# Weight halves in one tile, and one operand distance for every pass of a width

## The chip, the cores and the metric

The kernel runs on one core of a Trainium2 chip. The time is the device time of one execution in microseconds (us). The kernel before takes 2028.38 us, the median of three runs (2024.63 to 2029.26). The profile is of one execution on the chip. The engines are PE (TensorE, matrix products; PEld is its weight load), DVE (VectorE), ACT (ScalarE), POOL (GpSimd) and SP, which issues the transfers.

## The reference

One layer of a streaming encoder on 2048 tokens of width 1024, all float32: an RMSNorm, one input projection, two groups of heads, an output projection added to the input, a final RMSNorm.

```python
u = rmsnorm(h, norm_g[l])
proj = jnp.einsum('bsd,de->bse', u, w_in[l])
(q, k, v, o_pre, z_m, i_pre, f_pre,
 glu_a, glu_g, z_c) = jnp.split(proj, split_idx, axis=-1)
...
hm = mlstm_chunkwise(q, k, v, i_pre, f_pre)          # 4 heads of 256, matrix memory
hm = jax.nn.sigmoid(o_pre.astype(jnp.float32)) * hm
... # norm per head, times silu(z_m)
c = glu_a * jax.nn.sigmoid(glu_g)
... # causal depthwise convolution of width 31, LayerNorm, silu, times silu(z_c)
mix = jnp.concatenate([hm, c.astype(x.dtype)], axis=-1)
h = h + jnp.einsum('bse,ed->bsd', mix, w_out[l])
```

The input projection has 8 x 1024 + 8 columns, the output projection takes 2048 to 1024. These two are nearly all the work of PE.

## The kernel before

**Products in three passes.** To keep float32 accuracy each operand is split into a high half (rounded to the type fp32r) and a low half (the rest). A product of a weight slab and an activation tile is then three passes on PE: high weight with high activation, high weight with low activation, low weight with high activation (`products`, lines 324 to 353). Every pass is a weight load of a 128x128 stationary operand and a matmul that streams the moving operand past it, both read from SBUF.

**Units.** The tokens are done in two halves of 1024. In each half the projection is a list of units (`seq`), each of 256 columns of weights: `g` (convolution gate), `v`, `o`, `z`, `q`, `k` for four heads and `c`. A unit runs over eight blocks of 128 of the inner dimension. Units `g`, `q`, `k`, `c` (kind "fm", line 336) have the weights stationary and stream 512 tokens: 512 columns a pass. Units `o`, `z`, `v` (kind "tm2", line 343) have the tokens stationary and stream 256 weight columns. The first `v` unit of a half (kind "tm") streams 264 columns. The output projection (kind "tm", line 350) has the mixed tokens stationary and streams 512 weight columns, 8 units of 16 blocks, 12 passes a block.

**Where the operands lie.** An activation tile holds both halves one behind the other; `up` has 8 buffers of 2064 float32 (8256 bytes) a partition (`utiles`, line 271). The weight halves lie in two tiles, `wh` and `wl`, of 528 float32 (2112 bytes), four buffers each (`w_prep_`, line 213). 8256 and 2112 are both 64 more than a multiple of 256, so the place of a tile in a row of 256 bytes goes on by 64 bytes from buffer to buffer. In the built program activation tile j (counted modulo 8) begins at 24960 + 8256 x ((8 - j) mod 8), `wh` of slab i (counted modulo 4) at 91008 + 2112 x ((4 - i) mod 4), `wl` of it 8448 bytes further. Modulo 256 that is 128 - 64j for both halves of an activation tile and 128 - 64i for both halves of a slab. Columns within a tile are offsets of 512 or 1024 bytes in the units of 256 and 512 columns. So what is streamed and what is loaded stand 64 x (j - i) modulo 256 bytes apart where the weights are streamed, 64 x (i - j) where the tokens are, and all four distances (0, 64, 128, 192) take turns.

**Preparing a slab.** SP loads it (`w_load`), ACT writes the high half, POOL subtracts to get the low half, three slabs ahead of PE.

**The other work.** After the unit `k` of a head its eight chunks of 128 tokens (`mlstm`, `chunk`) run beside the later units, in steps s0 to s3: s0 makes the decayed scores `w` on DVE (line 633) from `sk` of PE and splits them, s1 does the products `num` and `kv` on PE (line 601), and the squares `sq` on ACT (line 699), s2 and s3 scale and transpose. The convolution is 31 taps of 128x1024 on DVE (line 787). A scheduler with a timeline simulation sets the order of the instructions on every engine; pools decide what must wait for a buffer to come free. A buffer of `bufs=1` that is shared under one tag makes each user wait for the one before.

Of the kernel before, what the change touches and what calls it, by code (L numbers as in the profile page):

```python
# [14 lines left out]
F32 = mybir.dt.float32  # L15
F32R = mybir.dt.float32r
# [3 lines left out]
P = 128  # L20
# [4 lines left out]
HD = 256  # L25
L = 128
NCH = HT // L
# [12 lines left out]
def hybrid_block_kernel(  # L40
# [14 lines left out]
    PUMP = 0.5  # L55
    WARM = 16

    PAD, ODD = 8, 0

    def pool(name, bufs, **kw):  # L60
        return ctx.enter_context(tc.tile_pool(name=name, bufs=bufs, **kw))
# [129 lines left out]
    wsrc = []  # L191
# [21 lines left out]
    def w_prep_(i):  # L213
        r, n = raws[i // 2]
        odd = wsrc[i // 2][2]
        s = r[:, (i % 2) * n : (i % 2 + 1) * n]
        hi = wp.tile([P, 528], F32R, tag="wh", name=f"wh{i}")
        lo = wp.tile([P, 528], F32R, tag="wl", name=f"wl{i}")
        hi, lo = hi[:, odd : odd + n], lo[:, odd : odd + n]
        nc.scalar.copy(hi, s)  # L220
        nc.gpsimd.tensor_tensor(out=lo, in0=s, in1=hi.bitcast(F32), op=ALU.subtract)  # L221
        wtile[i] = (hi, lo)
# [46 lines left out]
        return ps  # L269

    def utiles(key):
        odd = ODD if key[0][0] == "m" else 0
        both = up.tile([P, 2064], F32R, tag="u", name=f"u_{key[0]}_{key[1]}")
        h_, l_ = both[:, odd : odd + 1024], both[:, odd + 1024 : odd + 2048]
        uh[key], ul[key] = h_, l_
        return h_, l_

# [282 lines left out]
    def mlstm(hf, h):  # L560
# [46 lines left out]
        def chunk(c):  # L607
            tb, cc = c // 4, c % 4
            q, k = q_t[h, tb], k_t[h, tb]
            nm_ = f"{hf}_{h}_{c}"  # L610
            first = hf == 0 and c == 0
            sl = slice(cc * P, (cc + 1) * P)
            last = hf == 1 and c == NCH - 1
            v = [v_t[h, c // 2][:, i, c % 2, :] for i in range(2)]
            sg = oz_t[h, c // 2][:, 0, c % 2, :]
            sz = oz_t[h, c // 2][:, 1, c % 2, :]
            t = {}

            def s0():
                nm, ee = dec[tb]  # L620

                tc.keep_in_program_order(
                    nc.scalar.activation(ee[:, cc], ee[:, cc], AF.Exp, bias=a[:, h, c : c + 1])
                )
                sk = tp.tile([P, 512], F32, tag="tp", name=f"sk_{nm_}")
                for d in range(2):
                    nc.tensor.matmul(sk[:, :P], k[:, d, sl], q[:, d, sl], start=d == 0, stop=d == 1)

                if not last:
                    for d in range(2):  # L630
                        nc.tensor.transpose(sk[:, (d + 1) * P : (d + 2) * P], k[:, d, sl], ident)  # L631
                w = mlp.tile([P, P], F32, tag="w", name=f"w_{nm_}", bufs=1)
                nc.vector.scalar_tensor_tensor(  # L633
                    out=w, in0=sk[:, :P], scalar=rc[:, c : c + 1], in1=ee[:, cc], op0=ALU.mult, op1=ALU.mult
                )
                if not last:
                    kw = mlp.tile([P, 2, HD], F32R, tag="kw", name=f"kw_{nm_}")
                    wac = wa[:, h, c : c + 1]
                    nc.scalar.activation(kw[:, 0], sk[:, P : P + HD], AF.Identity, scale=wac)  # L639
                    nc.vector.scalar_tensor_tensor(  # L640
                        out=kw[:, 1], in0=sk[:, P : P + HD], scalar=wac, in1=kw[:, 0].bitcast(F32),
                        op0=ALU.mult, op1=ALU.subtract,
                    )
                    t["kw"] = kw
                t["w"] = halves(w, [P], "ws", nm_)
                if not first:
                    tc.keep_in_program_order(
                        nc.scalar.activation(nm[:, cc], nm[:, cc], AF.Exp, bias=bc[:, 0, h, c : c + 1])
                    )
                    qs = mlp.tile([P, 2, P], F32, tag="qs", name=f"qs_{nm_}", bufs=1)  # L650
                    nc.vector.tensor_tensor(
                        out=qs, in0=q[:, :, sl], in1=nm[:, cc : cc + 1, :].broadcast_to([P, 2, P]), op=ALU.mult
                    )
                    t["qs"] = halves(qs, [2, P], "qss", nm_)

            def state(d):
                if last:
                    return
                kv = acc.tile([P, 512], F32, tag="acc", name=f"kv_{nm_}_{d}")
                sd = slice(d * P, (d + 1) * P)  # L660
                kw = t["kw"]
                products3(kv[:, :VW], (kw[:, 0, sd], kw[:, 1, sd]), v, True, True)
                if first:
                    nc.vector.tensor_copy(cs[:, d], kv[:, :VW])
                else:
                    nc.vector.scalar_tensor_tensor(  # L666
                        out=cs[:, d], in0=cs[:, d], scalar=so[:, h, c : c + 1],
                        in1=kv[:, :VW], op0=ALU.mult, op1=ALU.add,
                    )
                if c == NCH - 1:  # L670
                    if d == 1:
                        nc.sync.dma_start(csc[h], cs)
                else:
                    state_split(d, nm_)

            def s1():
                num = acc.tile([P, 512], F32, tag="acc", name=f"num_{nm_}")
                products3(num[:, :VW], t["w"], v, True, first)
                if not first:
                    qh, ql = t["qs"]  # L680
                    for d in range(2):
                        products3(num[:, :VW], (qh[:, d], ql[:, d]), chl[d], False, d == 1)
                state(0)

                dn = sp.tile([P, 1], F32, tag="dn", name=f"dn_{nm_}")
                dc = num[:, HD : HD + 1]
                nc.vector.tensor_scalar(
                    out=dn, in0=dc, scalar1=-1.0, scalar2=en[:, h, c : c + 1], op0=ALU.mult, op1=ALU.max
                )
                nc.vector.tensor_tensor(out=dn, in0=dn, in1=dc, op=ALU.max)  # L690
                nc.vector.reciprocal(dn, dn)
                hm = mlp.tile([P, HD + 1], F32, tag="hm", name=f"hm_{nm_}")
                nc.gpsimd.memset(hm[:, HD:], EPS ** 0.5 * HD ** 0.5)
                nc.vector.scalar_tensor_tensor(
                    out=hm[:, :HD], in0=num[:, :HD], scalar=dn, in1=sg, op0=ALU.mult, op1=ALU.mult
                )
                sq = mlp.tile([P, HD + 1], mybir.dt.bfloat16, tag="sq", name=f"sq_{nm_}", bufs=1)
                ss = sp.tile([P, 1], F32, tag="ss", name=f"ss_{nm_}")
                nc.scalar.activation(sq, hm, AF.Square, scale=HD ** -0.5, accum_out=ss)  # L699
                nc.gpsimd.tensor_tensor(out=ss, in0=ss, in1=nhalf[:, 0:1], op=ALU.pow)  # L700
                t["hm"], t["ss"] = hm, ss

            def s2():
                state(1)
                hm = t["hm"][:, :HD]
                nc.vector.scalar_tensor_tensor(
                    out=hm, in0=hm, scalar=t["ss"], in1=sz, op0=ALU.mult, op1=ALU.mult
                )

            def s3():  # L710
                hm = t["hm"]
                mt = tp.tile([P, 512], F32, tag="tp", name=f"mt_{nm_}")
                for d in range(2):
                    nc.tensor.transpose(mt[:, d * P : (d + 1) * P], hm[:, d * P : (d + 1) * P], ident)  # L714
                if cc % 2 == 0:
                    dec["mo"] = k2p.tile([P, 2, 256], F32, tag="k2", name=f"mo_{nm_}")
                mo = dec["mo"]
                for d in range(2):
                    nc.scalar.activation(
                        mo[:, d, (cc % 2) * P : (cc % 2 + 1) * P], mt[:, d * P : (d + 1) * P],  # L720
                        AF.Identity, scale=col(V_MG, 2 * h + d),
                    )
                if cc % 2 == 1:
                    nc.sync.dma_start(
                        mixs[2 * hf + tb][:, 2 * h : 2 * h + 2, (cc - 1) * P : (cc + 1) * P], mo
                    )

            for i, fn in enumerate((s0, s1, s2, s3)):
                slots[SP * c + STG[i]].insert(0, fn)
# [191 lines left out]
    for hf in range(2):  # L921
# [7 lines left out]
        for u in s:  # L929
# [3 lines left out]
                        wsrc.append((wv0[g], 528, 0))  # L933
            else:
                for g in range(2):
                    wsrc.append((wu[WID[u], g], 512, 0 if u[0] in "ozv" else ODD))
    for b in range(4):
        for nn in range(2):
            for g in range(8):
# [16 lines left out]
    u_rstd(0)  # L956

    for hf in range(2):
        gt = gp.tile([P, NCH, 8], F32, tag="g_gt", name=f"gt{hf}", bufs=2)
        key = f"u{hf}"  # L960

        def opnd(kc, key=key):
# [164 lines left out]
```

## Time and profile before

| | |
|---|---|
| median of three runs | 2028.38 us |
| the profiled execution: its time, its span | 2027.2 us, 2025.5 us |
| PE busy, share of the span | 1994.9 us, 98% |
| weight loads (PEld) busy | 1748.2 us, 86% |
| DVE busy | 1430.9 us, 71% |
| ACT, POOL busy | 828.3 us, 801.2 us |
| mean granted clock of PE | 0.994 |

The 1.7 us between time and span lie before the first and after the last instruction. A matmul's own duration overlaps with the next one's (395 ns each for 512 columns, though one starts about every 230 ns), so what a pass costs is read from the distance of starts in the timeline, not from the mean duration.

### The profile page before, as it was taken

How to read it: one execution, taken by the hardware profiler on the slowest of the kernel's cores; microseconds unless marked ns; L12 is line 12 of the kernel's file. 1: busy time of each engine (PE TensorE's matmuls, PEld its weight loads, DVE VectorE, ACT ScalarE, POOL GpSimd, SP SyncE). 2: the span in 40 equal slices, each digit the busy share in tenths (PEclk: the TensorE clock that was granted, in tenths of full speed). 3: DMA queues.
4: the chain of work that ended last, by engine and by line, in shares of the span. 5: the costliest groups of instructions: out<-in, count | busy, mean ns of one | idle time of the engine just before them, and what ended most of it. 6: DMA issues, size and time to landing. Idle time of an engine off the chain costs nothing. (4 is left out here: it accounts for less than half of the span.)

```text
span 2025.5 us, 29786 instructions
## 1 busy us (share of the span) xinstructions
PE 1994.9 (98%) x11562; PEld 1748.2 (86%) x11562; DVE 1430.9 (71%) x1915; ACT 828.3 (41%) x1703; POOL 801.2 (40%) x740
## 2 busy tenths in 40 slices
PE   8999999999999999999999999999999999999998
PEld 7998998899899888888789879988998888788886
DVE  5598887689579755546799998977895658723231
ACT  5133532443343245535445225324423555543332
POOL 4532432343243232534333323423322326556464
PEclk9999999999999999999999999999999999999999
DMA  4211121112122233335311211211221566766452
GB/s 150 70 62 53 58 74 42 63 48 72 44 68 72 75 110 112 114 115 165 101 53 43 70 50 58 74 53 52 68 69 53 161 225 206 265 206 230 150 183 94
DMA packets 85837, 204.11 MB, mean 101 GB/s; under 512 B 7296, under 2 KB 40256, under 8 KB 85696
## 3 DMA queue, kind: packets, MB, share of 16 engines
q1 hardware_dynamic: 85696, 202.21, 30.5%
q8 instruction: 91, 1.49, 0.3%
q14 instruction: 50, 0.41, 0.1%
HBM read 159.15 MB, written 43.03 MB: 100 GB/s over the span
## 5 line engine op out<-in xcount | busy, mean ns | idle before, releaser
L221 POOL TENSOR_TENSOR wl<-wr,wh 128x512 fp32r<-128x512 f32 (+1 forms) x392 | 612.2, 1567 | 857.8 <-ACT wh L220 830.2
L336 PE MATMUL gm<-u_u,wh 128*128 128x512 f32 x2560 | 810.3, 395 | 1.8 <-DVE oz L451 0.9
L787 DVE SCALAR_TENSOR_TENSOR y<-c,vec,y 128x1024 f32<-128x1024 f32 x480 | 708.8, 1477 | 9.5
L336 PEld LDWEIGHTS gm<-u_u,wh 128*128 128x128 f32 x2560 | 477.3, 188 | 105.9 <-DVE oz L451 1.3
L336 PE MATMUL gm<-u_u,wl 128*128 128x512 f32 x1280 | 501.5, 394 | 0.0
L220 ACT CAST wh<-wr 128x512 fp32r<-128x512 f32 (+1 forms) x392 | 241.2, 619 | 598.4 <-PE gm L336 212.1
L343 PE MATMUL gm<-wh,u_u 128*128 128x256 f32 x2816 | 461.0, 282 | 5.5 <-DVE oz L451 3.4
L343 PEld LDWEIGHTS gm<-wh,u_u 128*128 128x128 f32 x2816 | 389.3, 190 | 7.2 <-DVE oz L451 3.6
L350 PE MATMUL gm<-wh,u_m 128*128 128x512 f32 x1024 | 319.7, 396 | 2.2 <-ACT wh L220 2.2
L336 PEld LDWEIGHTS gm<-u_u,wl 128*128 128x128 f32 x1280 | 240.9, 188 | 51.6 <-POOL wl L221 0.2
L343 PE MATMUL gm<-wl,u_u 128*128 128x256 f32 x1408 | 283.9, 282 | 0.0
L350 PEld LDWEIGHTS gm<-wh,u_m 128*128 128x128 f32 x1024 | 192.9, 189 | 46.6 <-ACT wh L220 2.5
L343 PEld LDWEIGHTS gm<-wl,u_u 128*128 128x128 f32 x1408 | 217.8, 190 | 0.1
L350 PE MATMUL gm<-wl,u_m 128*128 128x512 f32 x512 | 199.4, 396 | 0.5 <-POOL wl L221 0.5
L350 PEld LDWEIGHTS gm<-wl,u_m 128*128 128x128 f32 x512 | 96.5, 189 | 23.2 <-POOL wl L221 0.9
L700 POOL TENSOR_TENSOR ss<-ss,nhalf 128x1 f32<-128x1 f32 x64 | 53.5, 836 | 135.5 <-ACT sq L699 128.5
L1019 DVE TENSOR_TENSOR ht<-gm,ht 128x512 f32<-128x512 f32 x32 | 21.4, 688 | 118.5 <-PE gm L350 118.5
L281 DVE TENSOR_TENSOR u_m<-mr,u_m 128x1024 fp32r<-128x1024 f32 x32 | 43.9, 1371 | 76.6 <-ACT u_m L280 76.6
L633 DVE SCALAR_TENSOR_TENSOR w<-sk,rs,ee 128x128 f32<-128x128 f32 x64 | 22.1, 345 | 89.1 <-PE sk L631 84.4
L601 PE MATMUL kv<-v,kw 128*128 128x258 f32 x360 | 73.3, 289 | 0.6 <-DVE cs L666 0.6
L666 DVE SCALAR_TENSOR_TENSOR cs<-cs,g_so,kv 128x258 f32<-128x258 f32 x112 | 53.4, 477 | 24.8 <-PE kv L601 24.7
L639 ACT ACTIVATE kw<-sk,g_wa 128x256 fp32r<-128x256 f32 x60 | 28.3, 472 | 86.6 <-DVE w L633 86.6
(208 smaller groups left out, 2105.5 us busy)
## 6 DMA issues: line engine op xcount, KB each, us to landing
wr<-in_wu SPq DMA_DIRECT2D x123, 512.0 KB, 3.6
wr<-in_wo SPq DMA_DIRECT2D x64, 512.0 KB, 3.6
mr<-mixs SPq DMA_DIRECT2D x32, 512.0 KB, 4.5
ysc<-y SPq DMA_DIRECT2D x16, 512.0 KB, 2.6
mixs<-mo SPq DMA_DIRECT2D x32, 256.0 KB, 2.1
zsc<-zc SPq DMA_DIRECT2D x32, 256.0 KB, 2.1
ly<-ysc SPq DMA_DIRECT2D x16, 512.0 KB, 5.0
lz<-zsc SPq DMA_DIRECT2D x16, 512.0 KB, 5.7
```

The lines of the kernel that those rows point to most:

```text
L220: nc.scalar.copy(hi, s)
L221: nc.gpsimd.tensor_tensor(out=lo, in0=s, in1=hi.bitcast(F32), op=ALU.subtract)
L281: nc.vector.tensor_tensor(out=l_, in0=src, in1=h_.bitcast(F32), op=ALU.subtract)
L336: nc.tensor.matmul(ps[i], wt[:, o + cb * P : o + (cb + 1) * P], at[:, tb * 512 : (tb + 1) * 512], start=st, stop=sp_,)
L343: nc.tensor.matmul(ps[i][:, t2 * 256 : (t2 + 1) * 256], at[:, t * P : (t + 1) * P], wt[:, o : o + ncol], start=st and t2 == 0, stop=sp_, s ...
L350: nc.tensor.matmul(ps[i][:, :ncol], at[:, t * P : (t + 1) * P], wt[:, o : o + ncol], start=st, stop=sp_,)
L601: nc.tensor.matmul(ps, x_, y_, start=start and i == 0, stop=stop and i == 2)
L633: nc.vector.scalar_tensor_tensor(out=w, in0=sk[:, :P], scalar=rc[:, c : c + 1], in1=ee[:, cc], op0=ALU.mult, op1=ALU.mult)
L639: nc.scalar.activation(kw[:, 0], sk[:, P : P + HD], AF.Identity, scale=wac)
L666: nc.vector.scalar_tensor_tensor(out=cs[:, d], in0=cs[:, d], scalar=so[:, h, c : c + 1], in1=kv[:, :VW], op0=ALU.mult, op1=ALU.add,)
L700: nc.gpsimd.tensor_tensor(out=ss, in0=ss, in1=nhalf[:, 0:1], op=ALU.pow)
L787: tc.keep_in_program_order(nc.vector.scalar_tensor_tensor(out=y, in0=c[:, j + i * H2 : j + (i + 1) * H2], scalar=col(V_CW, b * CW + j), in1=y,
```

## The change

Both halves of a slab now lie in one tile `w` of 1152 float32 (4608 bytes, 18 x 256), the low half 2048 bytes behind the high half (2304 in the 264-column unit). The activation tile has 2048 float32 (8192 bytes, 32 x 256). In the built program activation tiles begin at 24960 + 8192n and weight tiles at 90496 + 4608n: all of them at 128 modulo 256. The units that stream 256 weight columns put their weights 48 float32 (192 bytes) into the tile. So in every pass of 512 columns the streamed and the loaded operand stand 0 modulo 512 bytes apart, and in every pass of 256 columns 192 modulo 512 (the streamed one ahead). In the first `v` unit it is 0 or 32 modulo 256.

Besides, `sq` of a chunk takes the one buffer of `w`, and the gate tile `gt` has one buffer in place of two. The scores tile `w` is one float32 longer.

```diff
-    PAD, ODD = 8, 0
+
+    PAD, ODD = 8, 48
...
-        hi = wp.tile([P, 528], F32R, tag="wh", name=f"wh{i}")
-        lo = wp.tile([P, 528], F32R, tag="wl", name=f"wl{i}")
-        hi, lo = hi[:, odd : odd + n], lo[:, odd : odd + n]
+        both = wp.tile([P, 1152], F32R, tag="w", name=f"w{i}")
+        o2 = 576 if n == 528 else odd + 512
+        hi, lo = both[:, odd : odd + n], both[:, o2 : o2 + n]
...
-        odd = ODD if key[0][0] == "m" else 0
-        both = up.tile([P, 2064], F32R, tag="u", name=f"u_{key[0]}_{key[1]}")
-        h_, l_ = both[:, odd : odd + 1024], both[:, odd + 1024 : odd + 2048]
+        both = up.tile([P, 2048], F32R, tag="u", name=f"u_{key[0]}_{key[1]}")
+        h_, l_ = both[:, :1024], both[:, 1024:]
...
-                w = mlp.tile([P, P], F32, tag="w", name=f"w_{nm_}", bufs=1)
+                w = mlp.tile([P, P + 1], F32, tag="w", name=f"w_{nm_}", bufs=1)[:, :P]
...
-                sq = mlp.tile([P, HD + 1], mybir.dt.bfloat16, tag="sq", name=f"sq_{nm_}", bufs=1)
+                sq = mlp.tile([P, HD + 2], mybir.dt.bfloat16, tag="w", name=f"sq_{nm_}", bufs=1)[:, : HD + 1]
...
-                    wsrc.append((wu[WID[u], g], 512, 0 if u[0] in "ozv" else ODD))
+                    wsrc.append((wu[WID[u], g], 512, ODD if u[0] in "ozv" else 0))
...
-        gt = gp.tile([P, NCH, 8], F32, tag="g_gt", name=f"gt{hf}", bufs=2)
+        gt = gp.tile([P, NCH, 8], F32, tag="g_gt", name=f"gt{hf}")
```

Every engine has as many instructions as before; the scheduler sets some of them in another order, most by a few places. One place is the second half, head 0, chunks 5 and 6 (`_1_0_5`, `_1_0_6`), on DVE. Before:

```order
L687 TENSOR_SCALAR dn_1_0_5_10621<-num_1_0_5_10602,g_en1_9379 128x1
L408 SCALAR_TENSOR_TENSOR v_1_1_1_10929<-gm_172_1_10539,rs_1_8272,v_1_1_1_10929 128x256
L633 SCALAR_TENSOR_TENSOR w_1_0_6_10669<-sk_1_0_6_10664,rs_1_8272,ee_1_0_1_10160 128x128
...
L640 SCALAR_TENSOR_TENSOR kw_1_0_6_10671<-sk_1_0_6_10664,g_wa1_9381,kw_1_0_6_10671 128x256
L592 TENSOR_TENSOR wsl_1_0_6_10675<-w_1_0_6_10669,wsh_1_0_6_10674 128x128
...
L694 SCALAR_TENSOR_TENSOR hm_1_0_5_10625<-num_1_0_5_10602,dn_1_0_5_10621,oz_1_0_2_9299 128x256
L787 SCALAR_TENSOR_TENSOR y_1_1_10163<-c_1_1_9007,vec_150,y_1_1_10163 128x1024
L706 SCALAR_TENSOR_TENSOR hm_1_0_5_10625<-hm_1_0_5_10625,ss_1_0_5_10629,oz_1_0_2_9299 128x256
```

Now:

```order
L691 RECIPROCAL dn_1_0_5_10445<-dn_1_0_5_10445 128x1
L787 SCALAR_TENSOR_TENSOR y_1_1_9992<-c_1_1_8856,vec_150,y_1_1_9992 128x1024
L694 SCALAR_TENSOR_TENSOR hm_1_0_5_10449<-num_1_0_5_10426,dn_1_0_5_10445,oz_1_0_2_9144 128x256
L787 SCALAR_TENSOR_TENSOR y_1_1_9992<-c_1_1_8856,vec_150,y_1_1_9992 128x1024
L633 SCALAR_TENSOR_TENSOR w_1_0_6_10492<-sk_1_0_6_10487,rs_1_8137,ee_1_0_1_9989 128x128
L706 SCALAR_TENSOR_TENSOR hm_1_0_5_10449<-hm_1_0_5_10449,ss_1_0_5_10453,oz_1_0_2_9144 128x256
L787 SCALAR_TENSOR_TENSOR y_1_1_9992<-c_1_1_8856,vec_150,y_1_1_9992 128x1024
L640 SCALAR_TENSOR_TENSOR kw_1_0_6_10494<-sk_1_0_6_10487,g_wa1_9225,kw_1_0_6_10494 128x256
L592 TENSOR_TENSOR wsl_1_0_6_10498<-w_1_0_6_10492,wsh_1_0_6_10497 128x128
```

The scores `w` of chunk 6 stood ahead of `hm` of chunk 5, from which `sq` of chunk 5 is made; now they stand behind it.

The second place is POOL, where the low halves of slabs 32 to 34 are made (the brackets name the engines and queues an instruction waits for). Before:

```order
L221 TENSOR_TENSOR wl32_1579<-wr16_1504,wh32_1578 128x512 [waits DMAHW0_49,PE_49,Activation_49]
L221 TENSOR_TENSOR wl33_1609<-wr16_1504,wh33_1608 128x512 [waits PE_49,Activation_49]
L221 TENSOR_TENSOR wl34_1642<-wr17_1576,wh34_1641 128x512 [waits DMAHW1_49,PE_49,Activation_49]
```

Now:

```order
L222 TENSOR_TENSOR w32_1546<-wr16_1474,w32_1546 128x512 [waits DMAHW0_49,Activation_49]
L222 TENSOR_TENSOR w33_1575<-wr16_1474,w33_1575 128x512 [waits Activation_49]
L222 TENSOR_TENSOR w34_1607<-wr17_1544,w34_1607 128x512 [waits DMAHW1_49,Activation_49]
```

POOL no longer waits for PE there: the ACT cast ahead of it takes over the wait, and waits for the last pass that reads the low half of the buffer's former slab, one pass later than the last that reads its high half.

## Rows read from the trace of the kernel before

**Rows 1.** The page: busy time, share of the span and instructions of each engine.

```profile
PE 1994.9 (98%) x11562; PEld 1748.2 (86%) x11562; DVE 1430.9 (71%) x1915; ACT 828.3 (41%) x1703; POOL 801.2 (40%) x740
```

**Rows 2.** Groups of PE by line and shape: busy time, mean ns, idle before.

```profile
L336 PE MATMUL gm<-u_u,wh 128*128 128x512 f32 x2560 | 810.3, 395 | 1.8 <-DVE oz L451 0.9 <-DVE g L759 0.3 <-DVE u_u L293 0.3
L336 PE MATMUL gm<-u_u,wl 128*128 128x512 f32 x1280 | 501.5, 394 | 0.0
L343 PE MATMUL gm<-wh,u_u 128*128 128x256 f32 x2816 | 461.0, 282 | 5.5 <-DVE oz L451 3.4 <-ACT oz L438 1.2 <-DVE v L408 0.8
L350 PE MATMUL gm<-wh,u_m 128*128 128x512 f32 x1024 | 319.7, 396 | 2.2 <-ACT wh L220 2.2
L343 PE MATMUL gm<-wl,u_u 128*128 128x256 f32 x1408 | 283.9, 282 | 0.0
L350 PE MATMUL gm<-wl,u_m 128*128 128x512 f32 x512 | 199.4, 396 | 0.5 <-POOL wl L221 0.5
```

**Rows 3.** Timeline of PE in the output projection: start, length, instruction.

```profile
1862.75 1.76 PE L350 MATMUL gm<-wh,u_m 128*128 128x512 f32 x7
1864.35 0.84 PE L350 MATMUL gm<-wl,u_m 128*128 128x512 f32 x3
1865.03 0.39 PE L350 MATMUL gm<-wh,u_m 128*128 128x512 f32 x1
...
1865.48 0.63 PE L350 MATMUL gm<-wh,u_m 128*128 128x512 f32 x2
...
1868.28 0.63 PE L350 MATMUL gm<-wh,u_m 128*128 128x512 f32 x2
...
1873.86 0.62 PE L350 MATMUL gm<-wh,u_m 128*128 128x512 f32 x2
...
1876.65 0.63 PE L350 MATMUL gm<-wh,u_m 128*128 128x512 f32 x2
...
1879.42 0.63 PE L350 MATMUL gm<-wh,u_m 128*128 128x512 f32 x2
```

**Rows 4.** Timeline of PE in a 256-column unit of the first half.

```profile
468.12 0.62 PE L343 MATMUL gm<-wh,u_u 128*128 128x256 f32 x4
...
470.17 0.63 PE L343 MATMUL gm<-wh,u_u 128*128 128x256 f32 x4
...
472.99 0.63 PE L343 MATMUL gm<-wh,u_u 128*128 128x256 f32 x4
...
475.83 0.63 PE L343 MATMUL gm<-wh,u_u 128*128 128x256 f32 x4
...
478.68 0.63 PE L343 MATMUL gm<-wh,u_u 128*128 128x256 f32 x4
...
481.41 0.64 PE L343 MATMUL gm<-wh,u_u 128*128 128x256 f32 x4
...
484.24 0.64 PE L343 MATMUL gm<-wh,u_u 128*128 128x256 f32 x4
...
487.12 0.63 PE L336 MATMUL gm<-u_u,wh 128*128 128x512 f32 x2
```

**Rows 5.** Window: length; busy us (count) of PE, PEld, DVE, ACT, POOL; clock, DMA.

```profile
1000.00:1250.00 250.00, 240.10 (x1458) 212.69 (x1457) 233.05 (x308) 96.16 (x218) 87.45 (x83) 0.99 0.17 55
```

**Rows 6.** Timeline, two pairs of a w on DVE and the sq before it on ACT.

```profile
1033.02 0.34 DVE L633 SCALAR_TENSOR_TENSOR w<-sk,rs,ee 128x128 f32<-128x128 f32 x1
...
1037.86 0.42 ACT L699 ACTIVATE sq<-hm 128x257 bf16<-128x257 f32 x1 [1.18 <-DVE hm L694]
...
1084.95 0.34 DVE L633 SCALAR_TENSOR_TENSOR w<-sk,rs,ee 128x128 f32<-128x128 f32 x1
...
1092.86 0.42 ACT L699 ACTIVATE sq<-hm 128x257 bf16<-128x257 f32 x1 [0.61 <-DVE hm L694]
```

**Rows 7.** Timeline, the closest pair in order: sq on ACT, then w on DVE.

```profile
774.13 0.41 ACT L699 ACTIVATE sq<-hm 128x257 bf16<-128x257 f32 x1
...
774.95 0.35 DVE L633 SCALAR_TENSOR_TENSOR w<-sk,rs,ee 128x128 f32<-128x128 f32 x1 [3.12 <-ACT ee L623]
```

## The prediction

> **What bounds the kernel now.** First the page: PE is busy 1994.9 us of the span of 2025.5, 98% [rows 1]; only 30.6 us are left in which it waits. A busy PE is not a PE at its peak, so the next view is the groups of PE by line and shape: 2560 + 1280 passes of 512 columns at L336 and 1024 + 512 at L350, together 5376, and 2816 + 1408 = 4224 of 256 columns at L343, with some 10 us of waiting ahead of all of them [rows 2]. The time of these 9600 passes is the time of the kernel; the question is what one pass takes, and the timeline of PE gives it from start to start.
>
> In the output projection a block is 12 passes, and its first row gives its start. Which distance a block has follows from the buffers of its tiles, and for the blocks that begin at 1862.75, 1865.48, 1876.65 and 1873.86 it is 0, 192, 64 and 128 bytes modulo 256. They take [rows 3]:
> - 0: 1865.48 - 1862.75 = 2.73 us, 227.5 ns a pass. It settles on the way: three passes between 1864.35 and 1865.03 take 0.68 us, 226.7 ns each.
> - 64: 1879.42 - 1876.65 = 2.77 us, 230.8 ns.
> - 128: 1876.65 - 1873.86 = 2.79 us, 232.5 ns.
> - 192: 1868.28 - 1865.48 = 2.80 us, 233.3 ns.
>
> Nothing else differs between these blocks: same line, same shape, no wait. So the distance of the two operands sets a part of the length of a pass. The mean of the four is 231.0 ns.
>
> In a unit of 256 columns I read six stretches of one distance each, of 24 passes (the first of 18) [rows 4]:
> - 64: 468.12 to 470.17, 113.9 ns; 470.17 to 472.99, 117.5 ns.
> - 128: 472.99 to 475.83, 118.3 ns; 475.83 to 478.68, 118.8 ns.
> - 192: 478.68 to 481.41, 113.8 ns; 481.41 to 484.24, 117.9 ns.
> - 0: 484.24 to 487.12, 120.0 ns.
>
> With 64 and 192 there are two paces at one distance: which one a stretch falls into is decided as it is entered, and it then stays. Means: 115.7, 118.5, 115.8, 120.0; over all four 117.5 ns.
>
> **The change part by part.**
>
> *512 columns.* All 5376 passes get distance 0. Before, a unit at L336 changes its distance with every activation tile, so no distance lasts long; now it lasts from unit to unit and is broken only where passes of `mlstm` (L601 and others) come between. A break costs a few passes until the rhythm is back, and the block of 12 at 227.5 ns contains such an entry. I take 227.5: (231.0 - 227.5) ns x 5376 = 18.8 us less. Ends: fully settled at 226.7 gives 4.3 x 5376 = 23.1 us; if the stretches at L336, cut by other passes, settle no better than the mean, nothing.
>
> *256 columns.* All 4224 passes get distance 192. Their mean is 115.8 if they fall into either pace equally often: (117.5 - 115.8) x 4224 = 7.2 us less. Ends: always the longer one, 117.9, 1.7 us more; always the shorter one, 113.8, 15.6 us less. I take the middle, because both occur in the one unit I read, next to each other.
>
> *The Trainium skill on this.* The blocks of [rows 3] differ by 6.6 ns a pass with nothing but the place of the operands. TensorE: Matmul & The Clock Gate (Part 2, what each phase is for) says that PE reads the moving operand and the next weights through two independent ports and that "loading the next tile's weights doesn't steal SBUF read bandwidth from the running matmul". By that rule the places of the operands could not matter and this part would be worth 0 in place of 18.8 + 7.2 us; the rows speak against it.
>
> *Other passes.* The 264-column passes (2 halves x 192 = 384) get distances of 0 or 32, and those of `mlstm` keep their tiles while the pool's places move by a few hundred bytes. No row separates distances there. With the spread of the 256-column passes, 113.8 to 120.0, as the bound, some 1300 such passes are worth up to 4 us either way; I take 0.
>
> *One tile for both halves of a slab.* The cast on ACT now waits for one more pass of the former slab, 0.23 us, and POOL for one wait less. A slab is made three ahead of PE, at least 2.7 us each [rows 3], and all waits of L350 for `wh` and `wl` are 2.7 us today [rows 2]. Cost 0; without that lead it would be 0.23 us for each of some 390 slabs, 90 us at the worst, which needs PE to stand at every slab as it does at almost none.
>
> *`sq` in the buffer of `w`.* The scores of a chunk may now be written only after the squares of the chunk before. Where the order is so already it costs nothing: the closest pair leaves 774.95 - (774.13 + 0.41) = 0.41 us [rows 7]. In three of 63 pairs it is not; two of them [rows 6] have `w` 5.3 us (1038.28 - 1033.02) and 8.3 us (1093.28 - 1084.95) ahead of the end of `sq`. There `w` moves behind `hm` on DVE, and what is queued behind it are the convolution taps and the splits that `num` on PE waits for. The scheduler has moved these too, and PE has passes of the next units to run meanwhile. So 0, bounded by the three waits in full, some 18 us (two read, the third taken as 5), and by a small gain below.
>
> *`gt` with one buffer.* Its second writing is half the kernel after its first; the cover is that the first half's gates are long done. 0, at most the length of a small DVE instruction.
>
> *Where PE is not alone.* Between 1000 and 1250 us PE is busy 240.1 of 250 us and DVE 233.1 [rows 5]: the convolution there is nearly as long as the products, and PE already waits 9.9 us. A faster PE would meet DVE there, so I count nothing for it: 250/2025 of 18.8 + 7.2 is 3.2 us.
>
> **Sum.** 18.8 + 7.2 - 3.2 = 22.8 us off the profiled execution's 2027.2 us: 2004.4. The median shown is 1.2 us above that execution, so 2005.6, and I say 2005.
>
> **The rivals.**
> - *Always the quicker pace.* With one distance throughout, the 256-column passes all fall into 113.8 ns. For: a stretch keeps its pace once it has it. Against: that holds for the longer one too, and each `mlstm` insertion throws the dice again. 22.8 + 15.6 - 7.2 = 31.2 us, 1997.
> - *DVE takes the place of PE.* What PE gains in the stages with much convolution turns into waits for evacuations on DVE. For: [rows 5]. Against: DVE is at 71% overall [rows 1]. Half of the gain gone: 2028.4 - 12 = 2016.
> - *`sq` and `w`.* The three late `w` show in full at `num`: 2005 + 18 = 2023. Against: the order moved with them.
> - *It does not do what it says.* The differences in [rows 3] have another cause that goes with the buffers, or hold only in undisturbed stretches: 2028. (The rule of independent ports in the Trainium skill, TensorE: Matmul & The Clock Gate, Part 2, would lead here too.)
> - *Slower: the constant distance is itself a collision.* In the trace before, the low weight half lies 8448 bytes behind the high one, 256 modulo 512, so a distance of 0 modulo 256 changes between 0 and 256 modulo 512 with the three passes. Now it is 0 modulo 512 every time, which no stretch in the trace shows. If both reads then meet in the same place pass after pass and settle at the slowest speeds read, 233.3 and 120.0, the passes lose 2.3 x 5376 + 2.5 x 4224 = 22.9 us: 2051. It decides the sign once the passes are longer than today's means of 231.0 and 117.5. Against: within a block two of three passes with the high weights follow each other at the same distance modulo 512, and the block at 0 is the fastest.
>
> **How the numbers follow.** The forecast has 0.62, the quicker pace 0.14, DVE 0.10, `sq` and `w` 0.04, no effect 0.05, collision 0.05. About 4 us (0.2%) is what a measurement can tell from no change; 2023 lies just beyond it and I split its chance. Faster: 0.62 + 0.14 + 0.10 + 0.02 = 0.88; same 0.05 + 0.02 = 0.07; slower 0.05. The range goes from 1993 (both widths fully settled: 23.1 + 15.6 - 3.2 = 35.5 us less) to 2016 (the DVE case).
>
> **What would show it.** Timeline: blocks of 12 passes in the output projection all at 2.72 to 2.73 us, whichever buffers they use; that stage about 230.8 against 227 ns a pass, some 6 us shorter for its 1536 passes. Stretches of 24 passes at L343 at 2.73 or 2.83 us, none at 2.88. PE still at 98% or a little less. Wrong would be blocks above 2.76 us (the distance is not it, or it collides), waits of `num` for `wsh` or `wsl` of several us (the shared buffer), or PE idle much beyond 31 us with DVE as releaser.

## The result, and the profile after

The kernel with the change takes 2010.92 us, the median of four runs (2007.46 to 2014.07), beside 2028.35 us of the kernel before on the same chip: a ratio of 0.9917, 95% interval 0.9893 to 0.9941. That is 17.4 us less. I had said 2005, between 1993 and 2016. The profiled executions differ by less, 2027.2 against 2014.07 us, 13.1 us; where the text compares traces, that is the difference to be explained. The gap between 13.1 and 17.4 goes with the granted clock of PE: the profiled execution after is the longest of its four, with a mean of 0.993, and the two at 2007.46 and 2008.25 us have 0.995; 0.002 of 2010 us is 4 us.

The page of the kernel after, busy time by engine, against [rows 1]:

```profile
PE 1975.9 (98%) x11562; PEld 1744.7 (87%) x11562; DVE 1445.4 (72%) x1915; ACT 827.7 (41%) x1703; POOL 792.3 (39%) x740
```

PE is busy 19.0 us less (1994.9 - 1975.9). Its idle time rose from 30.6 to 36.5 us (2012.4 of span - 1975.9), 5.9 us more, and the two make the 13.1. So there are two things to read: what the passes gained, and where PE now waits. (DVE is busy 14.5 us more with as many instructions; why was not tested.)

The passes first. The groups of PE by line and shape answer to [rows 2]; there is one group a line now, because both halves have the name `w`:

```profile
L336 PE MATMUL gm<-u_u,w 128*128 128x512 f32 x3840 | 908.6, 392 | 0.7 <-DVE u_u L293 0.6
L343 PE MATMUL gm<-w,u_u 128*128 128x256 f32 x4224 | 521.9, 281 | 5.7 <-DVE oz L451 3.4 <-ACT oz L438 1.7 <-DVE v L408 0.5
L350 PE MATMUL gm<-w,u_m 128*128 128x512 f32 x1536 | 355.0, 392 | 3.1 <-POOL w L222 1.9 <-DVE ht L1019 1.2
```

The timeline of PE (start, length, instruction; equal instructions in a row are one line) answers to [rows 3, 4]: two stretches at L343, one at L336 and one at L350.

```profile
115.77 16.60 PE L343 MATMUL gm<-w,u_u 128*128 128x256 f32 x144
...
456.63 26.63 PE L343 MATMUL gm<-w,u_u 128*128 128x256 f32 x224
...
499.67 30.54 PE L336 MATMUL gm<-u_u,w 128*128 128x512 f32 x134
...
1779.64 210.74 PE L350 MATMUL gm<-w,u_m 128*128 128x512 f32 x929
```

Take the last pass's own length off a line and divide by the passes ahead of it: (210.74 - 0.39)/928 = 226.7 ns, (30.54 - 0.39)/133 = 226.7 ns. What only the fastest block of before reached, 929 passes in a row now hold, over all buffers. At L343 there are two paces, as I had read them before: (16.60 - 0.28)/143 = 114.1 ns and (26.63 - 0.28)/223 = 118.2 ns. A stretch that nothing cuts keeps its pace; a unit that is cut by other passes can change it. The unit `o` of head 1 in the second half does, from 113.4 to 117.8 ns ((11.39 - 0.28)/98, begun in the unit before, and (9.23 - 0.28)/76):

```profile
1073.02 11.39 PE L343 MATMUL gm<-w,u_u 128*128 128x256 f32 x99
...
1089.73 9.23 PE L343 MATMUL gm<-w,u_u 128*128 128x256 f32 x77
```

From start to start over all passes that nothing interrupts (starts less than 1.15 times the median apart), the means are 231.36 -> 227.87 ns at L336, 117.74 -> 115.96 at L343, 231.31 -> 226.98 at L350. That is 3.49 x 3840 = 13.4 us, 1.78 x 4224 = 7.5 us and 4.33 x 1536 = 6.7 us, together 27.6 us gained in passes. The trace shows 13.1 less and the medians 17.4; 10 to 14.5 us were given back.

Where? I compare when PE starts the same unit of the program in both traces (after minus before, us, counted from the first pass of PE): 0.1 at 131 us, -4.0 at 482, -9.5 at 905, -10.5 at 1009, -6.2 at 1205, -12.5 at 1584, -8.7 at 1786, -13.3 at the end. The gain grows except in three places: the first 130 us, 1009 to 1205 us, and 1584 to 1786 us.

In the first it is mostly the clock. A window of it, before and after (length; busy us and count of PE, PEld, DVE, ACT, POOL; clock, DMA):

```profile
30.00:45.00 15.00, 11.58 (x78) 10.85 (x78) 8.00 (x13) 2.69 (x5) 4.75 (x4) 0.89 0.19 66
```

```profile
30.00:45.00 15.00, 11.91 (x69) 11.19 (x68) 7.06 (x11) 1.69 (x3) 3.95 (x4) 0.77 0.18 59
```

The granted clock stands at 1.2 GHz, half of its upper level, for 6.8 us here, before for 3.4, and PE starts 69 matmuls in place of 78. By the starts this costs 1.0 us of the 1.4 that the passes up to 131 us gain. A later run with the same order of matmuls, the one with many distances, has 0.89 and 81 matmuls here. Why the clock is low for longer is not shown.

The windows of before and after in the second place (length; busy us and count of PE, PEld, DVE, ACT, POOL; clock, DMA), [rows 5] being the wider one. Before:

```profile
1020.00:1212.00 192.00, 183.45 (x1139) 163.62 (x1138) 179.60 (x227) 72.35 (x163) 67.36 (x62) 0.98 0.18 57
```

After:

```profile
1000.00:1250.00 250.00, 239.57 (x1477) 213.75 (x1476) 233.60 (x317) 97.88 (x225) 87.73 (x85) 0.98 0.18 57
1020.00:1212.00 192.00, 181.70 (x1130) 162.73 (x1129) 181.09 (x230) 71.70 (x162) 69.19 (x64) 0.97 0.17 55
```

DVE is at 94% in this stretch (181.09 of 192) and PE starts fewer matmuls than before, 1130 against 1139, although each pass is shorter (the windows are at the same times, so the work in them is shifted by some 10 us). The granted clock is 0.97 of 2.4 GHz there in the mean, before 0.98: it is at 1.2 GHz for 10.2 us, before for 6.8. The waits of PE there, the longest of before and then of after (waited for, us in total, times, longest):

```profile
PE num L601 <- DVE qssl L592: 2.5, 1, 2.5
PE num L601 <- ACT wsh L591: 2.1, 1, 2.1
PE mt L714 <- DVE hm L706: 1.8, 1, 1.8
```

```profile
PE num L601 <- DVE qssl L592: 4.9, 4, 2.5
PE num L601 <- ACT wsh L591: 2.1, 2, 1.4
PE mt L714 <- DVE kw L640: 0.8, 1, 0.8
PE mt L714 <- DVE hm L706: 0.7, 1, 0.7
```

All waits listed there come to 8.6 us before (7 waits) and 10.1 after (12 waits). This view has only the time in which no matmul runs; by the starts the loss is larger. Starts over 1.15 times the usual distance of their shape apart, outside the stretches of 1.2 GHz, lose 12.7 us before and 17.4 after between the units at 1009 and 1205 us. One of the waits of after on the timeline, DVE and then PE:

```profile
1101.51 1.27 DVE L787 SCALAR_TENSOR_TENSOR y<-c,vec,y 128x1024 f32<-128x1024 f32 x1
1102.71 1.49 DVE L592 TENSOR_TENSOR qssl<-qs,qssh 128x256 fp32r<-128x256 f32 x1
1104.12 4.52 DVE L787 SCALAR_TENSOR_TENSOR y<-c,vec,y 128x1024 f32<-128x1024 f32 x2
```

```profile
1104.26 0.39 PE L601 MATMUL num<-c0h,qssl 128*128 128x258 f32 x1 [1.15 <-DVE qssl L592]
```

The split that `num` needs stands between convolution taps, DVE has no gap around it, and PE stands 1.15 us until it is done.

### The profile page after: what moved, and what is told of

It reads as the page before. It is cut to its first block, busy times and chain, and to the rows that moved or that the text cites. A ratio compares the mean times of both kernels' runs of the same rounds, so it can differ in the third digit from the quotient of the medians.

```text
span 2012.4 us, 29602 instructions
## 1 busy us (share of the span) xinstructions
PE 1975.9 (98%) x11562; PEld 1744.7 (87%) x11562; DVE 1445.4 (72%) x1915; ACT 827.7 (41%) x1703; POOL 792.3 (39%) x740
## 3 DMA queue, kind: packets, MB, share of 16 engines
q1 hardware_dynamic: 85696, 202.21, 30.6%
## 4 chain that ended last, share of the span: by engine, by line
PE 73%; DVE 18%; DMA 3%; issue 2%; ACT 2%; POOL 0%; SPq 0%; POOLq 0%; DVEq 0%; ACTq 0%
PE gm L336 32%; PE gm L343 18%; PE gm L350 16%; DVE y L787 11%; PE num L601 3%; PE kv L601 2%; PE sk L627 1%; DMA ly<-ysc 1%; DVE sm L302 1%; DMA wr<-in_wo 1%; PE mt L714 1%; DVE ly L844 1%; DMA ysc<-y 1%; PE sk L631 1%; ACT ly L881 0%
## 5 line engine op out<-in xcount | busy, mean ns | idle before, releaser
L222 POOL TENSOR_TENSOR w<-wr,w 128x512 fp32r<-128x512 f32 (+1 forms) x392 | 603.1, 1543 | 878.2 <-ACT w L221 859.4
L336 PE MATMUL gm<-u_u,w 128*128 128x512 f32 x3840 | 908.6, 392 | 0.7 <-DVE u_u L293 0.6
L336 PEld LDWEIGHTS gm<-u_u,w 128*128 128x128 f32 x3840 | 712.5, 188 | 143.2 <-DVE u_u L293 1.3
L343 PE MATMUL gm<-w,u_u 128*128 128x256 f32 x4224 | 521.9, 281 | 5.7 <-DVE oz L451 3.4
L343 PEld LDWEIGHTS gm<-w,u_u 128*128 128x128 f32 x4224 | 505.8, 190 | 7.6 <-DVE oz L451 3.6
L221 ACT CAST w<-wr 128x512 fp32r<-128x512 f32 (+1 forms) x392 | 241.4, 620 | 591.6 <-PE gm L336 200.2
L350 PE MATMUL gm<-w,u_m 128*128 128x512 f32 x1536 | 355.0, 392 | 3.1 <-POOL w L222 1.9
L350 PEld LDWEIGHTS gm<-w,u_m 128*128 128x128 f32 x1536 | 289.1, 189 | 64.2 <-POOL w L222 2.8
L601 PEld LDWEIGHTS kv<-v,kw 128*128 128x128 f32 x360 | 56.9, 190 | 3.2 <-DVE cs L666 0.6
L761 POOL TENSOR_TENSOR c<-c,g 128x512 f32<-128x512 f32 x32 | 40.9, 1284 | 30.4 <-ACT g L760 27.6
L350 PE MATMUL gm<-w,u_u 128*128 128x264 f32 x384 | 50.8, 294 | 0.0
```

What stands on the lines that cost most here:

```text
L336: nc.tensor.matmul(ps[i], wt[:, o + cb * P : o + (cb + 1) * P], at[:, tb * 512 : (tb + 1) * 512], start=st, stop=sp_,)
L343: nc.tensor.matmul(ps[i][:, t2 * 256 : (t2 + 1) * 256], at[:, t * P : (t + 1) * P], wt[:, o : o + ncol], start=st and t2 == 0, stop=sp_, s ...
L350: nc.tensor.matmul(ps[i][:, :ncol], at[:, t * P : (t + 1) * P], wt[:, o : o + ncol], start=st, stop=sp_,)
L601: nc.tensor.matmul(ps, x_, y_, start=start and i == 0, stop=stop and i == 2)
L761: nc.gpsimd.tensor_tensor(out=c[:, sl], in0=c[:, sl], in1=g, op=ALU.mult)
```

## The experiments

Two theories for what was given back. *A*: the added waits, `sq` in the buffer of `w`, cost it. *B*: DVE is the bound between 1000 and 1250 us (and wherever else it has the convolution), so shorter passes only make PE wait for it. Beside them stands the prediction's own mechanism, that the distance of the operands sets the length of a pass, with its rivals: no effect of the distance, or a collision at 0 modulo 512.

### The same program with other distances

Same code, same order of instructions on every engine, same buffers; only the offset of the weights in their tile is another. 512-column passes get a distance of 192 bytes, 256-column passes 0.

```diff
-    wsrc.append((wu[WID[u], g], 512, ODD if u[0] in "ozv" else 0))
+    wsrc.append((wu[WID[u], g], 512, 0 if u[0] in "ozv" else 16))
-    wsrc.append((wo[nn, g], 512, 0))
+    wsrc.append((wo[nn, g], 512, 48))
```

> The changed kernel with the same instructions in the same order on every engine; only the place of the weights in their tile differs, so that passes of 512 columns have the two operands 192 bytes apart modulo 256 and passes of 256 columns 0. Theory (the distance alone sets the length of a pass): the settled paces of the trace before, 233.3 ns and 120.0 ns, come back everywhere; against the changed kernel's 227.9 and 227.0 (L336, L350) and 116.0 ns that is 5.4 x 3840 + 6.3 x 1536 + 4.0 x 4224 = 47 us more pass time. If all of it shows, 2058 us; if DVE hides part of it in the second half, 2045 to 2058. Rival (the distance is not it; the new order of the instructions or the single tile is): within 0.3% of the changed kernel, 2011.

Measured: 2044.57 us (2043.08 to 2046.36), 1.0082 of the kernel before (1.0067 to 1.0098). Timeline of PE, as above:

```profile
467.45 27.12 PE L343 MATMUL gm<-w,u_u 128*128 128x256 f32 x224
...
499.78 30.50 PE L336 MATMUL gm<-u_u,w 128*128 128x512 f32 x130
...
1789.78 200.59 PE L350 MATMUL gm<-w,u_m 128*128 128x512 f32 x859
```

(200.59 - 0.40)/858 = 233.3 ns, (30.50 - 0.40)/129 = 233.3, (27.12 - 0.28)/223 = 120.4. These are the slow ends that I read in [rows 3, 4] for 192 and for 0. Nothing but the place of the operands differs from the kernel after, and the time differs by 33.7 us; the means of the passes account for 5.44 x 3840 + 3.76 x 4224 + 6.33 x 1536 = 46.5 us, of which a part is again not seen. The mechanism stands.

### The distances without the shared buffer, and the shared buffer without the distances

First the change with `sq` and `gt` as before (the weight tile is a little shorter, to make room; all distances as in the change modulo 256, but with this length they change between two values modulo 512):

```diff
-  both = wp.tile([P, 1152], F32R, tag="w", name=f"w{i}")
-  o2 = 576 if n == 528 else odd + 512
+  both = wp.tile([P, 1088], F32R, tag="w", name=f"w{i}")
+  o2 = 528 if n == 528 else odd + 512
...
-  w = mlp.tile([P, P + 1], F32, tag="w", name=f"w_{nm_}", bufs=1)[:, :P]
+  w = mlp.tile([P, P], F32, tag="w", name=f"w_{nm_}", bufs=1)
...
-  sq = mlp.tile([P, HD + 2], mybir.dt.bfloat16, tag="w", name=f"sq_{nm_}", bufs=1)[:, : HD + 1]
+  sq = mlp.tile([P, HD + 1], mybir.dt.bfloat16, tag="sq", name=f"sq_{nm_}", bufs=1)
...
-  gt = gp.tile([P, NCH, 8], F32, tag="g_gt", name=f"gt{hf}")
+  gt = gp.tile([P, NCH, 8], F32, tag="g_gt", name=f"gt{hf}", bufs=2)
```

> The distances of the changed kernel modulo 256, without its shared buffer: the weight tile has 1088 float32 in place of 1152, sq has its own buffer again and gt has two. The pitch of a weight tile is now 17 x 256 bytes, so distances change between 0 and 256 modulo 512. If only the distance modulo 256 counts, the passes are as in the changed kernel, 227.9, 227.0 and 116.0 ns; if the distance modulo 512 counts, they are longer. Theory A (the shared buffer of w and sq costs the missing part of the gain in the second half, some 7 us): 2003 to 2005. Theory B (DVE, nearly full between 1000 and 1250 us, takes it back whatever the buffers): 2008 to 2012, as the changed kernel, with the second half no shorter than before from its start to its unit 260.

Measured: 2013.69 us (2009.35 to 2013.8), 0.9926 (0.9913 to 0.9938). The same as the change within its interval. The means of the passes are those of the change too (227.63, 115.97 and 226.97 ns), so the distance modulo 512 makes no difference here. In the stage of DVE, this kernel:

```profile
1020.00:1212.00 192.00, 179.87 (x1126) 160.66 (x1125) 179.59 (x228) 71.46 (x161) 70.10 (x64) 0.98 0.17 57
```

No more matmuls than with the shared buffer (1126 against 1130). Then the kernel before with the shared buffer alone:

```diff
-  w = mlp.tile([P, P], F32, tag="w", name=f"w_{nm_}", bufs=1)
+  w = mlp.tile([P, P + 1], F32, tag="w", name=f"w_{nm_}", bufs=1)[:, :P]
...
-  sq = mlp.tile([P, HD + 1], mybir.dt.bfloat16, tag="sq", name=f"sq_{nm_}", bufs=1)
+  sq = mlp.tile([P, HD + 2], mybir.dt.bfloat16, tag="w", name=f"sq_{nm_}", bufs=1)[:, : HD + 1]
```

> The kernel before with nothing changed but w and sq in one buffer. Theory A (the shared buffer costs): 4 to 8 us slower than before, 2032 to 2036, lost between the second and third head of the second half. Theory B (it costs nothing, DVE is the limit): within 2 us of before. Passes as before, 231.4 and 117.7 ns.

Measured: 2029.15 us, 1.0007 (0.9999 to 1.0016). Theory A falls twice. In the kernel after, DVE waits for a free buffer of `w` once in 64 chunks:

```profile
DVE w L633 <- ACT sq L699: 1.6, 1, 1.6
```

### Many distances in one run

Each unit of the kernel after gets another offset.

```diff
+  TM2 = iter([0, 16, 32, 48, 8, 24, ...])
+  FM = iter([0, 4, 8, 12, 16, 20, ...])
...
+  at = next(TM2 if u[0] in "ozv" else FM)
-  wsrc.append((wu[WID[u], g], 512, ODD if u[0] in "ozv" else 0))
+  wsrc.append((wu[WID[u], g], 512, at))
```

> The changed kernel with the same instructions in the same order; every unit of the projection has its weights at another place in the tile: 22 distances for the 256-column units (steps of 16 bytes over 256, then some beyond 256 and one of 4 and one of 8 bytes), 40 for the 512-column units. It measures the pace of a pass by distance. Theory (a period of 256 bytes): the pace depends on the distance modulo 256 alone, 226.7 at 0 and 233.3 at 192 for 512 columns, 120.0 at 0 and 113.8 or 117.9 at 64 and 192 for 256 columns, and distances 256 apart agree within 1 ns. Rival (a period of 512 or of 64): distances 256 apart differ, or those 64 apart agree. Its time lies between the changed kernel and before, 2010 to 2035.

Measured: 2025.78 us, one run, between the other two, as a mixture should be. Timeline of PE, four stretches at L336 with distances of 96, 80, 32 and 16 bytes:

```profile
487.99 20.24 PE L336 MATMUL gm<-u_u,w 128*128 128x512 f32 x86
...
509.70 20.64 PE L336 MATMUL gm<-u_u,w 128*128 128x512 f32 x89
...
665.92 20.45 PE L336 MATMUL gm<-u_u,w 128*128 128x512 f32 x87
...
687.61 20.57 PE L336 MATMUL gm<-u_u,w 128*128 128x512 f32 x90
```

233.5, 230.1, 233.3 and 226.7 ns. Over all units, with 512 columns: 226.7 ns at 16 and, where it settles, at 0; 230.0 at 80; 229.1 to 229.7 at 64, but 233.3 at the start of two of its three units; 226.6 in one stretch at 240 and 233.3 in the others; 232 to 234 at 32, 48, 96, 112, 128, 144, 160, 176, 192, 208 and 224. A distance and the same plus 256 give the same: 226.7 ns at 0 and at 256, 230.0 at 80 and at 336, 232.8 at 128 and at 384, 233.3 at 192 and at 448. So the period is 256 bytes as far as these pairs go. That 0 modulo 512 is no collision the kernel after shows itself, with 226.7 ns over 929 passes: that rival falls. With 256 columns: 113.3 to 114.4 at best (64, 112, 192), 120.0 at 0, 123.2 at 4, between 116.7 and 126 within one unit at 8, two paces for several.

### Less convolution in the second half

B says that the gain comes back where DVE has less to do. In the second half 10 of the 30 taps that follow the first are left out, in the kernel before, in the kernel after, and in the one with the other distances.

```diff
-  for j in range(1, CW):
+  for j in range(1, 21 if hf else CW):
```

> The kernel before with 20 in place of 31 taps of the convolution in the second half of the tokens (10 to 11 taps of 1.48 us on DVE left out for each of 8 blocks, some 118 us of DVE work; the output is not the reference's). It is the partner of the next two runs. If DVE holds PE up between 1000 and 1200 us, its waits there (some 10 us) go: 2015 to 2021. If not, 2028.

> The changed kernel with 20 taps in the second half in the same way. The passes save 27.5 us between the two kernels (3.5 ns x 3840, 4.3 x 1536, 1.8 x 4224). Theory B (DVE, nearly full early in the second half, gave the rest back): the second half now keeps its share, some 10 us between the starts of its first unit and of its last one, where the full kernels show 1; the whole is 20 to 24 us below the partner before. Rival (the new order of the instructions gave it back, whatever DVE's load): again about 1 us over those units, and 15 to 18 us in all.

> The kernel of e1 (distances 192 and 0) with 20 taps in the second half; instructions and order are those of the changed kernel with 20 taps. Between e1 and the changed kernel the passes differ by 46 us and the time by 34. Theory B: with DVE relieved the two differ by 40 to 46 us. Rival (the rest of the difference is lost elsewhere): 34 again.

Measured: 2020.8 us (2019.45 to 2023.23), 1996.71 (1993.21 to 1997.95) and 2036.31 (2033.78 to 2037.77). From before to after the change is now worth 24.1 us, where it was 17.4, while the passes gain the same (231.27 -> 227.81, 117.67 -> 115.98, 231.30 -> 226.95 ns). From the good to the bad distances it is 39.6 where it was 33.7. The scheduler orders the instructions anew when taps are left out, so the first comparison changes the order along with DVE's work. The second is free of that: within each of its pairs every engine has one and the same order, and of passes that differ by 46.5 and 46.7 us more is seen once DVE has less to do. The window of the stage, before with 20 taps:

```profile
1000.00:1250.00 250.00, 243.80 (x1518) 218.21 (x1517) 202.32 (x300) 101.97 (x235) 87.46 (x90) 0.99 0.17 58
```

After with 20 taps:

```profile
1000.00:1250.00 250.00, 246.24 (x1592) 223.30 (x1590) 205.05 (x309) 105.56 (x244) 83.25 (x94) 0.99 0.17 58
```

DVE is at 81 to 82%, and PE starts 74 matmuls more in the same time, where with all taps it was 19 more (1477 against 1458). The starts of the units tell it by place (after minus before, both with 20 taps): -10.9 at the unit where it was -10.5, -13.7 where it was -6.2, -16.0 where it was -12.5, -18.1 where it was -8.7, -22.7 at the end where it was -13.3. The gain now grows through both later places at which it was lost. The loss at long starts between the units at 1009 and 1205 us, 12.7 and 17.4 us above, is 8.6 before and 7.8 after. B is shown for 1009 to 1205 us, as far as what is given back there goes away with DVE's work. That the place behind 1584 us recovers too says that it hangs on the convolution as well; which of its waits does it, the runs don't separate (after, PE waits there for `w` of POOL 1.9 us, `ht` 1.2, `dg_l` 1.1, `lq` 1.0, and before only 2.7 for slabs and 0.3).

### Better distances

From the list of distances I took 112 for the 256-column passes, and 16 for those of 512.

```diff
-  wsrc.append((wu[WID[u], g], 512, ODD if u[0] in "ozv" else 0))
+  wsrc.append((wu[WID[u], g], 512, 28 if u[0] in "ozv" else 60))
-  wsrc.append((wo[nn, g], 512, 0))
+  wsrc.append((wo[nn, g], 512, 4))
```

> The changed kernel with the same order and distances of 16 bytes for 512 columns and 112 for 256 columns, which e4 showed at 226.7 ns with no slow entry and at 113.7 ns in all its long stretches. If these hold everywhere, the passes save a further 1 ns x 3840 and 1.5 to 2 ns x 4224, 10 to 12 us; with the same share given back as before, 6 to 8 us below the changed kernel: 2003 to 2006. If 112 has a second pace that one unit did not show, or 16 behaves as 0 once passes of other kinds cut in, within 2 us of the changed kernel.

Measured: 2011.76 us (2007.98 to 2012.81), 0.9917 (0.9903 to 0.9932), no better than the change. Timeline of PE:

```profile
1789.70 200.55 PE L350 MATMUL gm<-w,u_m 128*128 128x512 f32 x865
```

(200.55 - 0.39)/864 = 231.7 ns at L350, where the weights are streamed, though 16 gave 226.7 at L336. Nor did L336 keep that: the unit that had 226.7 ns at 16 in the run with many distances has (21.40 - 0.39)/92 = 228.4 here, at the same offset in its tile.

```profile
679.77 21.40 PE L336 MATMUL gm<-u_u,w 128*128 128x512 f32 x93
```

So the distance alone doesn't say it all at 16. What else decides, which operand is streamed, where it lies or how a stretch begins, is open. The 256-column passes did improve, 115.96 to 114.75 ns. Then 112 with the distance 0 of the change for 512 columns:

```diff
-  wsrc.append((wu[WID[u], g], 512, ODD if u[0] in "ozv" else 0))
+  wsrc.append((wu[WID[u], g], 512, 28 if u[0] in "ozv" else 0))
```

> The changed kernel with the same order and distances of 0 for all passes of 512 columns and 112 for those of 256. In e8 the 256-column passes took 114.75 ns at 112 against 115.96 at 192, while 16 was worse than 0 for 512 columns. If the paces hold, the passes save 1.2 ns x 4224 = 5.1 us against the changed kernel; with about two thirds of it showing, 3 us: 2006 to 2009. Rival (DVE and the waits take all of it): as the changed kernel, 2011.

Measured: **2006.36 us** (2005.24 to 2007.44), 0.9893 (0.9878 to 0.9908), the shortest of all with the whole computation. The unit that had 118.2 ns above:

```profile
456.96 25.71 PE L343 MATMUL gm<-w,u_u 128*128 128x256 f32 x224
```

(25.71 - 0.28)/223 = 114.0 ns. The mean, 114.74, makes (115.96 - 114.74) x 4224 = 5.2 us, and 4.6 less is seen.

### Some of DVE's work to POOL

B suggests to take work off DVE. The low halves of the states are made on POOL (on top of the last kernel).

```diff
-  nc.vector.tensor_tensor(out=lo, in0=f, in1=hi.bitcast(F32), op=ALU.subtract)
+  eng = nc.gpsimd if tag in ("c0", "c1") else nc.vector
+  eng.tensor_tensor(out=lo, in0=f, in1=hi.bitcast(F32), op=ALU.subtract)
```

> e9 with the low half of the mLSTM states (c0l, c1l: some 120 subtractions of 0.42 us on DVE) made on POOL. Theory B (DVE holds PE up early in the second half): some 25 us of DVE work less in that half, 3 to 6 us below e9, with fewer waits of num for DVE between 1000 and 1200 us. Rival: POOL takes longer for each (its 128x512 subtraction is 1.5 us), num waits for POOL instead, and the time is e9's or above.

Measured: 2020.38 us (2019.24 to 2022.35), 0.9965 (0.9952 to 0.9977): 14 us *more* than without it. The window of the stage, first of the last kernel and then of this one; waits of PE over the whole run; and the groups of the moved instructions on POOL:

```profile
1000.00:1250.00 250.00, 239.10 (x1491) 213.61 (x1490) 233.47 (x319) 98.06 (x226) 87.22 (x86) 0.98 0.17 56
```

```profile
1000.00:1250.00 250.00, 231.14 (x1403) 204.72 (x1402) 221.55 (x280) 99.42 (x221) 107.79 (x107) 0.97 0.16 52
```

```profile
PE num L602 <- ACT qssh L591: 5.4, 5, 2.0
PE num L602 <- DVE qssl L593: 4.1, 4, 2.5
```

```profile
L593 POOL TENSOR_TENSOR c1l<-cs,c1h 128x258 fp32r<-128x258 f32 x56 | 50.1, 894 | 65.7 <-ACT c1h L591 65.3
L593 POOL TENSOR_TENSOR c0l<-cs,c0h 128x258 fp32r<-128x258 f32 x56 | 48.5, 866 | 81.8 <-ACT c0h L591 81.5
```

DVE has less to do in the stage, 221.6 us against 233.5, and PE does less all the same, 1403 matmuls against 1491. The subtraction takes 866 to 894 ns on POOL in the mean (its medians are 747 and 710, on DVE 421 and 420), it stands in the chain from state to `num`, and the order of all engines moved with it. So the sum of DVE's work alone does not decide. That it is how late DVE's (or POOL's) links of that chain come is argued and not shown: leaving taps out makes every link earlier, moving a link does not. Besides, the granted clock is lower, 0.991 in the mean against 0.993 of the last kernel: it stands at 1.2 GHz for 10.2 us more, worth at most 5.1 us. Which part of the 14 us is POOL's length and which the new order was not separated.

## Why the prediction was right, and which term was mis-sized

- *512 columns, 18.8 us: right.* Measured 13.4 + 6.7 = 20.1. The rhythm settles fully at L350 and nearly so at L336, where 227.87 holds what the breaks by `mlstm` cost. The mean of four blocks [rows 3], 231.0, stood for all 5376 passes within 0.4 ns.
- *256 columns, 7.2 us: right.* Measured 7.5. Both paces occur at the one distance: of the 56 stretches of more than 12 passes that nothing cuts, 33 have 113.3 to 114.4 ns and 23 have 117.6 to 118.5, and none takes 120. (The prediction speaks of six stretches and lists seven; its means are right.) The rival "always the quicker pace" did not come; the run with 112 bytes comes closer to it.
- *The rule of independent ports (the Trainium skill, TensorE: Matmul & The Clock Gate, Part 2).* It would have given 0. The run with other distances has the same instructions in the same order and takes 33.7 us more; measurement decides against the rule for this use.
- *Collision at 0 modulo 512, 2051: wrong*, as the 226.7 ns over 929 passes at that distance show.
- *`sq` and `w`, the cast and `gt`, all taken as 0: right.* The shared buffer alone is 1.0007; PE waits for slabs at L350 1.9 us where it was 2.7; `gt` was only tried together with `sq`.
- *"Where PE is not alone", 3.2 us: the step that failed, in its size.* I let the stage between 1000 and 1250 us give nothing and counted the rest in full. Shown is 10 to 14.5 us given back. From start to start the 9600 passes took 19.4 us less in all, of the 27.6 that their pace gives, and PE's other matmuls took 6.0 us more; that makes the 13.4 us by which the starts of all 11562 draw together, near the 13.1 seen. Between 1009 and 1205 us the stage did not merely gain nothing; it became 4.3 us longer (191.7 to 196.0 us), where PE came 10.5 us earlier into a stage in which DVE is at 94%. The usual distances of what PE runs there come to 1.2 us less, long starts lost 4.7 us more (12.7 to 17.4), and 3.4 us more at 1.2 GHz cost 0.9. The moved order has a share in the 4.7: the run with the other distances has the order of after with longer passes, and loses 15.2 us at long starts there. So by one trace of each about half came with the order and half with the shorter passes; with 20 taps neither shows (8.6 before, 7.8 after, 8.6 with the other distances). Behind 1584 us another 3.8 us went, also gone with fewer taps. The first 130 us gained nothing, mostly because of 3.4 us more at 1.2 GHz.

The result lies halfway between the forecast, 2005, and the rival "DVE takes the place of PE", 2016. Its mechanism was there; I gave it a tenth, because DVE's 71% of the whole span spoke against it. What counts is its 93% in the stage [rows 5] and its 81% with 20 taps, at which 24.1 us are seen, between the 22.8 of my sum and the 26.0 ahead of the deduction.

Of what I had said the profile would show, blocks at 2.72 us (12 x 226.7 ns), stretches at 2.74 and 2.84 us (24 x 114.1 and 118.2) and none at 2.88 came; so did, in a mild form, what I had named as a sign of being wrong: PE idle for 36.5 us, with DVE as the releaser of most of what was added (15.8 us of waits before, 20.7 after).

## What to carry to other kernels

Where every pass loads its weights anew, look at the distance between streamed and loaded operand modulo 256 bytes: start to start, the same pass took from 226.7 to 234 ns with 512 columns and from 113.3 to 126 with 256, and a constant good distance is had for an offset in the tile. Try the distances in one run, a unit each, before choosing, and confirm each at the line where it will stand. And where the second engine is at 93%, a gain of the first can be worth less than nothing: the stage here became 4.3 us longer, with a share of the clock and of the new order in it. So read the waits, the clock and the order of that stage.

## What had not been expected of the hardware

- A distance of 16 bytes gives 226.7 ns a pass in one run and 228.4 in the same unit of another, both with the tokens streamed, and 231.7 with the weights streamed.
- At one distance (192) 256-column passes run at 114.1 ns over 144 passes or 118.2 over 224, and one unit changes from 113.4 to 117.8; at 112 the unit read above has 114.0.
- The same 128x258 subtraction that has a median of 420 ns on DVE has one of 710 to 747 on POOL, and moving it cost 14 us, though DVE was the engine PE waited for.
